# Stick-breaking attention on one NeuronCore: two heads' scores on the two row halves of the matrix array, and one scan over 1280 columns per head

## The chip, the cores and the metric

The kernel runs on one core of one Trainium2 chip. The core has a matrix engine (TensorE, PE in the profile; its weight loads are listed apart as PEld), a vector engine (VectorE, DVE), an activation engine (ScalarE, ACT), a general engine (GpSimd, POOL) and a queue from which most transfers are started (SyncE, SP). Each engine works through its own list of instructions in order. Engines wait for one another through semaphores. Matrix products go to PSUM, which has eight banks of 512 fp32 columns here, and DVE and ACT take them from there to SBUF.

The metric is the device time of one execution in microseconds (us); shorter is better.

## The reference

The program is one layer of a decoder on 512 tokens of width 1024. A normalised input is projected into queries, keys and values of 8 heads of 64, three convolution inputs and two gates. Attention and a gated convolution are mixed, followed by an MLP of width 4096 and a per-layer gate. The part that the change touches is the attention, cut to this (z are the scores of 128 queries against all keys, 4 such blocks):

```
z = einsum('bhqd,bhkd->bhqk', q_block, k) * 64 ** -0.5
causal = key_pos < q_pos
log_beta = log_sigmoid(z)
log_keep = where(causal, log_beta - z, 0)
between = cumsum(log_keep, axis=3, reverse=True) - log_keep
w = where(causal, exp(log_beta + between), 0)
out = einsum('bhqk,bhkd->bhqd', w, v)
```

So the weight of a key is beta = sigmoid(z), times the product of keep = sigmoid(-z) over all later keys that the query may see. The products are taken by a scan from the last key to the first.

## The kernel before

All large products are made from fp32 values that are split in two: `split` (lines 63 to 66) lets ACT copy the value rounded to a shorter format ("hi") and DVE subtract that from the value ("lo"). A product is then three matmuls in one PSUM bank, hi by hi, hi by lo and lo by hi (`mm3`, lines 89 to 92).

Scores have only 64 rows to contract, half of the array's 128. Before, `proj_q` makes for each head a tile `st` with q hi in one half of the rows and q lo in the other. `proj_k` writes k hi into both halves, and k lo into both halves, of the same tile. A score block is then two matmuls over all 128 rows: [q hi; q lo] by [k hi; k hi] (line 338), and [q hi; q lo] by [k lo; k lo] (line 339), which also adds the product lo by lo. This takes six 64-row copies on ACT (lines 315, 317, 325) and six 64-row subtractions on DVE (lines 316, 318, 326) for a pair of heads.

`scores` handles one head. Its keys are cut causally: query block 3 sees 512 columns, block 2 sees 384, block 1 sees 256, block 0 sees 128, together 1280 columns that lie side by side in the tiles `beta` and `keep` (the table `BLK`). ACT makes beta and keep from PSUM in three groups of columns (512, 384 + 128, 256; lines 341 and 342). POOL sets the diagonal blocks (line 347, one 128x128 select for beta and one for keep per query block). For each query block DVE then scans keep backwards (line 350) and multiplies beta by the shifted result (line 351).

The loop over j (line 424, four turns, two heads each) has this order on PE: scores of both heads; `conv_u` and `conv_b` (24 matmuls of 512 columns each); `wtrans` of the first head's weights (ten 128x128 transposes, line 366, which need that head's finished beta); the next q projection; `wtrans` of the second head; the next k projection; two `av`; and the next `conv_c`. In the last turn gates stand in place of the projections. PE and SP run in exactly the written order. For ACT, DVE and POOL a scheduler that works with modelled times and the priorities in the code (`high_priority(-LATE)` marks work that may come late) sets the order when the program is built. Tiles come from pools of a fixed number of buffers: `big` has 16, the weights pool `wts` 15, raw weights 4, PSUM 8.

In the profile every matmul of `mm3` has line 90, 91 or 92, and every split line 64 (ACT) or 65 (DVE), whoever calls them.

Of the kernel before, what the change touches and what calls it, by code (L numbers as in the profile page):

```python
# [16 lines left out]
P = 128  # L17
S = 512
# [10 lines left out]
BLK = {3: (0, 512), 2: (512, 384), 0: (896, 128), 1: (1024, 256)}  # L29
# [4 lines left out]
def hybrid_block(ctx, tc, x, p, g_pre_mix, w_in, b_gate, w_conv, w_attn_out, w_conv_out, w_o,  # L34
                 g_post_mix, g_pre_mlp, w_up, w_down, g_post_mlp, g_ple, w_ple_gate, w_ple_proj, out):
    nc = tc.nc
# [4 lines left out]
    w_in, w_conv, w_attn_out, w_conv_out = w_in[0], w_conv[0], w_attn_out[0], w_conv_out[0]  # L41
# [12 lines left out]
    def bigt(shape, dt=F32R, name="big"):  # L54
        return big.tile(shape, dt, tag="big", name=name)

    def bank():
        return psp.tile([P, 512], F32, tag="ps", name="ps")

    def tm(dt=F32):  # L60
        return tmp.tile([P, 512], dt, tag="tmp", name="tmp")

    def split(hi, lo, src):
        a = nc.scalar.copy(hi, src)  # L64
        b = nc.vector.tensor_tensor(lo, src, hi.bitcast(F32), op=ALU.subtract)  # L65
        return a, b

    def weights(loads, shape):
        raw = raws.tile(shape, F32, tag="raw", name="raw")
        for sel, src in loads(raw):  # L70
            nc.sync.dma_start(sel, src)
        lo = wts.tile(shape, F32R, tag="w", name="wlo")
        hi = wts.tile(shape, F32R, tag="w", name="whi")
        half = shape[1] // 2
        for sl in (slice(0, half), slice(half, 2 * half)):
            split(hi[:, sl], lo[:, sl], raw[:, sl])
        return hi, lo
# [4 lines left out]
    def wcols(w, c0):  # L82
        src = w[:, c0:c0 + P].rearrange("(k p) m -> p k m", p=P)
        return weights(lambda t: [(t, src)], [P, NK, P])
# [4 lines left out]
    def mm3(ps, lh, ll, rh, rl, start, stop, onto=False):  # L89
        nc.tensor.matmul(ps, lh, rh, start=start, stop=False, skip_group_check=onto)  # L90
        nc.tensor.matmul(ps, lh, rl, start=False, stop=False, skip_group_check=onto)  # L91
        nc.tensor.matmul(ps, ll, rh, start=False, stop=stop, skip_group_check=onto)  # L92

    def proj(w, xs, nk=NK, k0=0):
        ps = bank()
        for k in range(nk):
            xh, xl = xs(k)
            mm3(ps, w[0][:, k0 + k], w[1][:, k0 + k], xh, xl, k == 0, k == nk - 1)
        return ps
# [47 lines left out]
    def mov(hp):  # L147
        return lambda k: (hp[0][k // 4][:, k % 4, :], hp[1][k // 4][:, k % 4, :])
# [119 lines left out]
    for t in range(2, NT):  # L268
        ps = bank()
# [11 lines left out]
    hx = mov(h1)  # L281
# [27 lines left out]
        unsaved.extend([(dst[:, 0:2], o[0]), (dst[:, 2:4], o[1])])  # L309


    def proj_q(j):
        a, b = st = [bigt([P, 3, S], name="st") for _ in range(2)]
        ps = proj(wcols(w_in, j * P), hx)
        nc.scalar.copy(a[0:64, 0], ps[0:64])
        nc.vector.tensor_tensor(a[64:128, 0], ps[0:64], a[0:64, 0].bitcast(F32), op=ALU.subtract)
        nc.scalar.copy(b[64:128, 0], ps[64:128])
        nc.vector.tensor_tensor(b[0:64, 0], ps[64:128], b[64:128, 0].bitcast(F32), op=ALU.subtract)
        return st

    def proj_k(j, st):
        ps = proj(wcols(w_in, 512 + j * P), hx)
        for s_, r, o in ((st[0], slice(0, 64), slice(64, 128)), (st[1], slice(64, 128), slice(0, 64))):
            for d in (r, o):
                nc.scalar.copy(s_[d, 1], ps[r])
                nc.vector.tensor_tensor(s_[d, 2], ps[r], s_[r, 1].bitcast(F32), op=ALU.subtract)

    def scores(st):
        beta = bigt([P, 1280], F32, "beta")
        keep = bigt([P, 1280], F32, "keep")  # L330
        for group in ((3,), (2, 0), (1,)):
            ps = bank()
            base = BLK[group[0]][0]
            for qb in group:
                c0, n = BLK[qb]
                c0 -= base
                lhs = st[:, 0, qb * P:(qb + 1) * P]
                nc.tensor.matmul(ps[:, c0:c0 + n], lhs, st[:, 1, 0:n], start=True, stop=False)  # L338
                nc.tensor.matmul(ps[:, c0:c0 + n], lhs, st[:, 2, 0:n], start=False, stop=True)  # L339
            n = sum(BLK[qb][1] for qb in group)  # L340
            nc.scalar.activation(beta[:, base:base + n], ps[:, 0:n], AF.Sigmoid, scale=0.125)
            nc.scalar.activation(keep[:, base:base + n], ps[:, 0:n], AF.Sigmoid, scale=-0.125)
        for qb in (3, 2, 0, 1):
            c0, n = BLK[qb]
            dg = slice(c0 + n - P, c0 + n)
            for t_, fill in ((beta, 0.0), (keep, 1.0)):
                nc.gpsimd.affine_select(t_[:, dg], t_[:, dg], pattern=[[-1, P]], compare_op=ALU.is_gt,
                                        fill=fill, base=0, channel_multiplier=1)
            kr = keep[:, c0:c0 + n][:, ::-1]
            nc.vector.tensor_tensor_scan(kr, kr, kr, 1.0, op0=ALU.mult, op1=ALU.bypass)  # L350
            nc.vector.tensor_tensor(beta[:, c0:c0 + n - 1], beta[:, c0:c0 + n - 1], keep[:, c0 + 1:c0 + n],
                                    op=ALU.mult)
        return beta

    def wtrans(w):
        wh = bigt([P, 1280], name="wth")
        wl = bigt([P, 1280], name="wtl")
        for group in ((0,), (1, 3), (2,)):
            ps = bank()
            base = WBLK[group[0]][0]  # L360
            n = 0
            for kb in group:
                c0 = WBLK[kb][0] - base
                for qb in range(kb, NT):
                    o = BLK[qb][0] + kb * P
                    nc.tensor.transpose(ps[:, c0 + (qb - kb) * P:c0 + (qb - kb + 1) * P], w[:, o:o + P], ident)  # L366
                n += WBLK[kb][1]
            split(wh[:, base:base + n], wl[:, base:base + n], ps[:, 0:n])
        return wh, wl
# [19 lines left out]
    def conv_c(c):  # L389
        ps = proj(wcols(w_in, 2048 + c * P), hx)  # L390
        ct = tm()
        nc.scalar.copy(ct, ps)
        return ct

    def conv_u(c, ct):
        ps = proj(wcols(w_in, 2560 + c * P), hx)
        nc.vector.tensor_tensor(ct, ct, ps, op=ALU.mult)
        y = tm()
        wc = [cols[:, 16 + i * 4 + c:17 + i * 4 + c] for i in range(3)]
        nc.vector.tensor_scalar(y, ct, wc[2], None, op0=ALU.mult)  # L400
        for i, d in ((1, 1), (0, 2)):
            nc.vector.scalar_tensor_tensor(y[:, d:S], ct[:, 0:S - d], wc[i], y[:, d:S], op0=ALU.mult, op1=ALU.add)
        return y

    def conv_b(c, y):
        ps = proj(wcols(w_in, 1536 + c * P), hx)
        nc.vector.tensor_tensor(y, ps, y, op=ALU.mult)
        split(oy_h[1][:, c], oy_l[1][:, c], y)

    def gate(j, which):  # L410
        ps = proj(wcols(w_in, 3072 + 1024 * which + j * P), hx)
        sg = tm()
        nc.scalar.activation(sg, ps, AF.Sigmoid, bias=cols[:, 8 * which + j:8 * which + j + 1])
        return sg

    with tc.high_priority(-LATE):
        make_sums(nc.vector)
    st = proj_q(0)
    with tc.high_priority(-LATE):
        make_sums(nc.vector)  # L420
    proj_k(0, st)
    ct = conv_c(0)
    sg = [None, None]
    for j in range(4):
        wa = scores(st[0])
        wb = scores(st[1])
        y = conv_u(j, ct)
        conv_b(j, y)
        ta = wtrans(wa)
        if j < 3:  # L430
            st = proj_q(j + 1)
        else:
            sg[0] = gate(0, 0)
        tb = wtrans(wb)
        if j < 3:
            proj_k(j + 1, st)
        else:
            sg[1] = gate(0, 1)
        of = tm()
        if j in (1, 2):  # L440
# [20 lines left out]
    for j in range(NK):  # L461
# [28 lines left out]
        if j == 7:  # L490
            for kk in range(2):
                ps = bank()
# [382 lines left out]
    for t in range(2, NT):  # L875
        for cs in CUTS[t]:
            ps = bank()[:, 0:cs.stop - cs.start]
# [31 lines left out]
```

## Time and profile before

| what | value |
|---|---|
| time, median of 3 executions | 736.56 us (735.95 to 737.09) |
| the profiled execution | 737.48 us |
| its span, first to last instruction | 735.7 us |
| PE busy | 727.5 us (99%) |
| DVE busy | 538.4 us (73%) |
| ACT busy | 392.4 us (53%) |
| POOL busy | 89.2 us (12%) |
| granted TensorE clock | 1.000 |
| the four turns of the attention loop | 52.8 to about 195 us of the span |

The timeline view gives for each piece its start, its duration, the engine, the line, the operation with its operands' names and sizes, how many instructions it merges (x4), and in brackets the idle time of the engine before it with what ended it. A matmul's listed duration is a model of its whole way through the array; consecutive matmuls overlap, so the step from one start to the next is what a matmul costs in a stream. The windows view gives for stretches of the span their length and the busy time and count of each engine. The difference of 1.8 us between time and span is what lies around the first and last instruction.

### The profile page before, as it was taken

To read this page: it belongs to the slowest core of one execution; us is meant where nothing else is said; L and a number is where in the kernel's file an instruction comes from. 1 tells how busy PE (TensorE), PEld (TensorE's weight loads), DVE (VectorE), ACT (ScalarE), POOL (GpSimd) and SP (SyncE) were. 2 spreads that over 40 slices of the span, in tenths; PEclk is the share of its full clock that TensorE was granted. 3 is DMA by queue.
4 is the path that set the end of the run, shared out by engine and by line. 5 is a ranking of instruction groups with operands and counts; after the bars stand their busy time and mean duration, and the time that the engine had idled before them with its cause. 6 is when DMAs were issued, how large, how long until landed. Compare 5 with 4: busy or idle time off the path is not lost.

```text
span 735.7 us, 10417 instructions
## 1 busy us (share of the span) xinstructions
PE 727.5 (99%) x3944; PEld 631.4 (86%) x3944; DVE 538.4 (73%) x740; ACT 392.4 (53%) x647; POOL 89.2 (12%) x119
## 2 busy tenths in 40 slices
PE   8999999999999999999999999999999999999997
PEld 7878888888888888888899999999988888888886
DVE  6779898989545533844789898976799878269762
ACT  6264746373434221443856696757767477256431
POOL 1005041323332222001100000000000000001100
PEclk9999999999999999999999999999999999999999
DMA  8591717174798967862325544523555767577311
GB/s 314 170 290 57 218 40 229 62 224 141 234 341 256 279 207 261 296 216 70 152 94 170 176 115 115 148 81 107 153 171 178 219 249 226 177 242 270 128 57 58
DMA packets 112106, 132.29 MB, mean 180 GB/s; under 512 B 4116, under 2 KB 82744, under 8 KB 111032
## 3 DMA queue, kind: packets, MB, share of 16 engines
q1 hardware_dynamic: 111464, 127.43, 54.8%
q10 hardware_dynamic: 592, 4.20, 1.4%
q8 instruction: 31, 0.51, 0.3%
q14 instruction: 19, 0.16, 0.1%
HBM read 108.55 MB, written 23.07 MB: 179 GB/s over the span
## 4 chain that ended last, share of the span: by engine, by line
PE 85%; DVE 6%; DMA 5%; issue 1%; ACT 1%; SPq 0%; POOL 0%; POOLq 0%; DVEq 0%; ACTq 0%
PE ps L90 27%; PE ps L92 27%; PE ps L91 26%; DMA raw<-in_w_up_dram 3%; DMA raw<-in_w_in_dram 2%; DVE us L65 2%; PE ps L380 1%; PE ps L366 1%; PE ps L339 1%; PE ps L181 1%; PE ps L338 1%; PE ps L565 1%; PE ps L140 0%; DVE s L660 0%; DVE wlo L65 0%
## 5 line engine op out<-in xcount | busy, mean ns | idle before, releaser
L65 DVE TENSOR_TENSOR wlo<-raw,whi 128x512 fp32r<-128x512 f32 x120 | 84.8, 737 | 42.7 <-ACT whi L64 20.9
L90 PE MATMUL ps<-h1h,whi 128*128 128x512 f32 x288 | 113.0, 392 | 0.0
L92 PE MATMUL ps<-h1h,wlo 128*128 128x512 f32 x288 | 112.3, 390 | 0.0
L91 PE MATMUL ps<-h1l,whi 128*128 128x512 f32 x288 | 112.2, 390 | 0.0
L64 ACT CAST whi<-raw 128x512 fp32r<-128x512 f32 x120 | 68.9, 630 | 48.5 <-DMA raw<-in_w_in_dram 15.8
L90 PE MATMUL ps<-w,sb 128*128 128x512 f32 x216 | 84.1, 389 | 0.0
L92 PE MATMUL ps<-w,sb 128*128 128x512 f32 x216 | 84.0, 389 | 0.0
L91 PE MATMUL ps<-w,sb 128*128 128x512 f32 x216 | 84.0, 389 | 0.0
L65 DVE TENSOR_TENSOR w<-raw,w 128x1024 fp32r<-128x1024 f32 x56 | 67.6, 1221 | 21.5 <-ACT w L64 10.4
L64 ACT CAST w<-raw 128x1024 fp32r<-128x1024 f32 x56 | 58.4, 1052 | 36.1 <-DMA raw<-wsum 14.4
L132 POOL TENSOR_TENSOR rs<-ms,mhalf 128x1 f32<-128x1 f32 x20 | 14.2, 712 | 419.6 <-DVE ms L128 365.7
L90 PE MATMUL ps<-h2h,us 128*128 128x256 f32 x224 | 63.5, 283 | 0.4 <-DVE tmp L692 0.4
L92 PEld LDWEIGHTS ps<-h1h,wlo 128*128 128x128 f32 x288 | 54.1, 188 | 11.3
L91 PEld LDWEIGHTS ps<-h1l,whi 128*128 128x128 f32 x288 | 54.1, 188 | 10.8
L91 PE MATMUL ps<-h2l,us 128*128 128x256 f32 x224 | 63.4, 283 | 0.0
L92 PE MATMUL ps<-h2h,us 128*128 128x256 f32 x224 | 63.4, 283 | 0.0
L90 PEld LDWEIGHTS ps<-h1h,whi 128*128 128x128 f32 x288 | 54.1, 188 | 10.8
L65 DVE TENSOR_TENSOR us<-raw,us 128x1024 fp32r<-128x1024 f32 x42 | 50.6, 1219 | 5.9 <-ACT us L64 5.8
L64 ACT CAST us<-raw 128x1024 fp32r<-128x1024 f32 x42 | 43.3, 1049 | 17.0 <-DVE raw L664 8.5
L91 PEld LDWEIGHTS ps<-w,sb 128*128 128x128 f32 x216 | 40.6, 188 | 8.4
L92 PEld LDWEIGHTS ps<-w,sb 128*128 128x128 f32 x216 | 40.6, 188 | 8.4
L90 PE MATMUL ps<-tb,us 128*128 128x256 f32 x168 | 47.7, 284 | 0.0
(210 smaller groups left out, 1693.1 us busy)
## 6 DMA issues: line engine op xcount, KB each, us to landing
raw<-in_w_in_dram SPq DMA_DIRECT2D x36, 512.0 KB, 6.5
w<-in_w_down_dram SPq DMA_DIRECT2D x32, 512.0 KB, 4.5
wsum<-w SPq DMA_DIRECT2D x32, 512.0 KB, 4.1
raw<-in_w_up_dram SPq DMA_DIRECT2D x32, 512.0 KB, 4.6
raw<-wsum SPq DMA_DIRECT2D x32, 512.0 KB, 5.0
raw<-in_w_down_dram SPq DMA_DIRECT2D x24, 512.0 KB, 4.2
raw<-in_w_o_dram SPq DMA_DIRECT2D x8, 512.0 KB, 5.7
raw<-in_w_ple_gate_dram SPq DMA_DIRECT2D x8, 512.0 KB, 7.1
```

Source lines behind the costliest of these rows:

```text
L64: a = nc.scalar.copy(hi, src)
L65: b = nc.vector.tensor_tensor(lo, src, hi.bitcast(F32), op=ALU.subtract)
L90: nc.tensor.matmul(ps, lh, rh, start=start, stop=False, skip_group_check=onto)
L91: nc.tensor.matmul(ps, lh, rl, start=False, stop=False, skip_group_check=onto)
L92: nc.tensor.matmul(ps, ll, rh, start=False, stop=stop, skip_group_check=onto)
L132: nc.gpsimd.tensor_tensor(r, m, mhalf, op=ALU.pow)
L181: nc.tensor.transpose(warm[:, 0:P], ident, ident)
L338: nc.tensor.matmul(ps[:, c0:c0 + n], lhs, st[:, 1, 0:n], start=True, stop=False)
L339: nc.tensor.matmul(ps[:, c0:c0 + n], lhs, st[:, 2, 0:n], start=False, stop=True)
L366: nc.tensor.transpose(ps[:, c0 + (qb - kb) * P:c0 + (qb - kb + 1) * P], w[:, o:o + P], ident)
L380: nc.tensor.matmul(ps[:, kb * P:S], lhs, wt[i][:, c0:c0 + n], start=(kb == 0 and i == 0), stop=(kb == NT - 1 and i == 1))
L565: nc.tensor.transpose(ps[:, i * P:(i + 1) * P], hn1[t][g][:, i * P:(i + 1) * P], ident)
```

## The change

q and k are each split once, as one 128-row copy and one 128-row subtraction, into a tile `st` of four parts (q hi, q lo, k hi, k lo). The first head of the pair lies in rows 0 to 63, the second in rows 64 to 127. `scores` handles both heads. Each score block is three matmuls per head with 64 contracted rows (hi by hi, hi by lo, lo by hi), issued alternately for the head in the upper and the head in the lower rows, into two banks. The three column groups of both heads so take six banks. Lo by lo is no longer computed. ACT makes beta and keep of both heads group by group.

A constant tile `ends` holds 1 in the last column of each query block and 0 elsewhere. The scan now goes over all 1280 columns of a head at once: the running product is multiplied by keep, and then the larger of it and `ends` is taken, which starts it again at 1 at each block's last key (where keep has just been set to 1). One multiplication over 1279 columns replaces four; the column at each block's end takes part, where beta is zero on the diagonal.

```diff
     def proj_q(j):
-        a, b = st = [bigt([P, 3, S], name="st") for _ in range(2)]
-        ps = proj(wcols(w_in, j * P), hx)
-        nc.scalar.copy(a[0:64, 0], ps[0:64])
-        nc.vector.tensor_tensor(a[64:128, 0], ps[0:64], a[0:64, 0].bitcast(F32), op=ALU.subtract)
...
+        st = bigt([P, 4, S], name="st")
+        split(st[:, 0], st[:, 1], proj(wcols(w_in, j * P), hx))
         return st

     def proj_k(j, st):
-        ps = proj(wcols(w_in, 512 + j * P), hx)
-        for s_, r, o in ((st[0], slice(0, 64), slice(64, 128)), (st[1], slice(64, 128), slice(0, 64))):
-            for d in (r, o):
-                nc.scalar.copy(s_[d, 1], ps[r])
-                nc.vector.tensor_tensor(s_[d, 2], ps[r], s_[r, 1].bitcast(F32), op=ALU.subtract)
+        split(st[:, 2], st[:, 3], proj(wcols(w_in, 512 + j * P), hx))
...
-                lhs = st[:, 0, qb * P:(qb + 1) * P]
-                nc.tensor.matmul(ps[:, c0:c0 + n], lhs, st[:, 1, 0:n], start=True, stop=False)
-                nc.tensor.matmul(ps[:, c0:c0 + n], lhs, st[:, 2, 0:n], start=False, stop=True)
+                for i, (a, b) in enumerate(((0, 2), (0, 3), (1, 2))):
+                    for h in range(2):
+                        r = slice(64 * h, 64 * h + 64)
+                        nc.tensor.matmul(ps[h][:, c0:c0 + n], st[r, a, qb * P:(qb + 1) * P], st[r, b, 0:n],
+                                         start=i == 0, stop=i == 2)
...
-            kr = keep[:, c0:c0 + n][:, ::-1]
-            nc.vector.tensor_tensor_scan(kr, kr, kr, 1.0, op0=ALU.mult, op1=ALU.bypass)
-            nc.vector.tensor_tensor(beta[:, c0:c0 + n - 1], beta[:, c0:c0 + n - 1], keep[:, c0 + 1:c0 + n],
-                                    op=ALU.mult)
+            kr = keep[h][:, ::-1]
+            nc.vector.tensor_tensor_scan(kr, kr, ends[:, ::-1], 1.0, op0=ALU.mult, op1=ALU.max)
+            nc.vector.tensor_tensor(beta[h][:, 0:1279], beta[h][:, 0:1279], keep[h][:, 1:1280], op=ALU.mult)
...
-        wa = scores(st[0])
-        wb = scores(st[1])
+        wa, wb = scores(st)
```

The scheduler orders ACT, DVE and POOL anew. On ACT, in the second turn of the loop, this is the part from the last copy before the scores to the casts behind them. `beta_868` and `keep_869` are the first head's tiles, `beta_911` and `keep_912` the second's; `whi` are hi parts of weights that PE uses a turn later. Before:

```order
L392 COPY tmp_866<-ps_841 128x512
L341 ACTIVATE beta_868<-ps_870 128x512
L342 ACTIVATE keep_869<-ps_870 128x512
L341 ACTIVATE beta_868<-ps_875 128x512
L342 ACTIVATE keep_869<-ps_875 128x512
L341 ACTIVATE beta_868<-ps_882 128x256
L342 ACTIVATE keep_869<-ps_882 128x256
L341 ACTIVATE beta_911<-ps_913 128x512
```

Now (`beta_852` and `keep_854` belong to the first head, `beta_853` and `keep_855` to the second):

```order
L392 COPY tmp_850<-ps_825 128x512
L64 CAST whi_1318<-raw_1315 128x512 x2
L342 ACTIVATE beta_852<-ps_856 128x512
L343 ACTIVATE keep_854<-ps_856 128x512
L342 ACTIVATE beta_853<-ps_857 128x512
L343 ACTIVATE keep_855<-ps_857 128x512
L64 CAST whi_1376<-raw_1373 128x512
L342 ACTIVATE beta_852<-ps_868 128x512
L343 ACTIVATE keep_854<-ps_868 128x512
L342 ACTIVATE beta_853<-ps_869 128x512
L343 ACTIVATE keep_855<-ps_869 128x512
L342 ACTIVATE beta_852<-ps_886 128x256
```

Three weight casts stand ahead of or among the activations, and the first head's last piece comes ninth and tenth of twelve where it came fifth and sixth. The first and third turn read alike; in the fourth no cast stands between the copy and the last activation.

On DVE, in the same turn, from the last weight subtraction ahead of the first scan to the first convolution product. Before, part of the first head:

```order
L350 SCALAR_TENSOR_TENSOR keep_869<-keep_869 128x512
L351 TENSOR_TENSOR beta_868<-beta_868,keep_869 128x511
L350 SCALAR_TENSOR_TENSOR keep_869<-keep_869 128x384
L350 SCALAR_TENSOR_TENSOR keep_869<-keep_869 128x128
L351 TENSOR_TENSOR beta_868<-beta_868,keep_869 128x383
L351 TENSOR_TENSOR beta_868<-beta_868,keep_869 128x127
L350 SCALAR_TENSOR_TENSOR keep_869<-keep_869 128x256
L350 SCALAR_TENSOR_TENSOR keep_912<-keep_912 128x512
L351 TENSOR_TENSOR beta_868<-beta_868,keep_869 128x255
```

Now, all of both heads (a scan is named SCALAR_TENSOR_TENSOR here):

```order
L65 TENSOR_TENSOR wlo_1317<-raw_1315,whi_1318 128x512 x2
L351 SCALAR_TENSOR_TENSOR keep_854<-keep_854,ends_383 128x1280
L351 SCALAR_TENSOR_TENSOR keep_855<-keep_855,ends_383 128x1280
L352 TENSOR_TENSOR beta_852<-beta_852,keep_854 128x1279
L352 TENSOR_TENSOR beta_853<-beta_853,keep_855 128x1279
L397 TENSOR_TENSOR tmp_850<-tmp_850,ps_942 128x512
```

Both scans stand ahead of both multiplications, so the first head's weights are finished behind the second head's scan. All four turns have this order.

More of the change, by code (lines that the diff above doesn't have):

```diff
@@ L309, in make_sums @@
         unsaved.extend([(dst[:, 0:2], o[0]), (dst[:, 2:4], o[1])])
+    ends = bigt([P, 1280], F32, "ends")
+    nc.gpsimd.memset(ends, 0.0)
+    for c0, n in BLK.values():
+        nc.gpsimd.memset(ends[:, c0 + n - 1:c0 + n], 1.0)
     def proj_q(j):
-        a, b = st = [bigt([P, 3, S], name="st") for _ in range(2)]
-        ps = proj(wcols(w_in, j * P), hx)
-        nc.scalar.copy(a[0:64, 0], ps[0:64])
-        nc.vector.tensor_tensor(a[64:128, 0], ps[0:64], a[0:64, 0].bitcast(F32), op=ALU.subtract)
-        nc.scalar.copy(b[64:128, 0], ps[64:128])
-        nc.vector.tensor_tensor(b[0:64, 0], ps[64:128], b[64:128, 0].bitcast(F32), op=ALU.subtract)
+        st = bigt([P, 4, S], name="st")
+        split(st[:, 0], st[:, 1], proj(wcols(w_in, j * P), hx))
         return st
     def proj_k(j, st):
-        ps = proj(wcols(w_in, 512 + j * P), hx)
-        for s_, r, o in ((st[0], slice(0, 64), slice(64, 128)), (st[1], slice(64, 128), slice(0, 64))):
-            for d in (r, o):
-                nc.scalar.copy(s_[d, 1], ps[r])
-                nc.vector.tensor_tensor(s_[d, 2], ps[r], s_[r, 1].bitcast(F32), op=ALU.subtract)
+        split(st[:, 2], st[:, 3], proj(wcols(w_in, 512 + j * P), hx))
     def scores(st):
-        beta = bigt([P, 1280], F32, "beta")
-        keep = bigt([P, 1280], F32, "keep")
+        beta = [bigt([P, 1280], F32, "beta") for _ in range(2)]
+        keep = [bigt([P, 1280], F32, "keep") for _ in range(2)]
         for group in ((3,), (2, 0), (1,)):
-            ps = bank()
+            ps = [bank(), bank()]
             base = BLK[group[0]][0]
@@ L336, in scores @@
                 c0 -= base
-                lhs = st[:, 0, qb * P:(qb + 1) * P]
-                nc.tensor.matmul(ps[:, c0:c0 + n], lhs, st[:, 1, 0:n], start=True, stop=False)
-                nc.tensor.matmul(ps[:, c0:c0 + n], lhs, st[:, 2, 0:n], start=False, stop=True)
-            n = sum(BLK[qb][1] for qb in group)
-            nc.scalar.activation(beta[:, base:base + n], ps[:, 0:n], AF.Sigmoid, scale=0.125)
-            nc.scalar.activation(keep[:, base:base + n], ps[:, 0:n], AF.Sigmoid, scale=-0.125)
@@ L343, in scores @@
[L343 to L348, printed above, removed]
-            kr = keep[:, c0:c0 + n][:, ::-1]
-            nc.vector.tensor_tensor_scan(kr, kr, kr, 1.0, op0=ALU.mult, op1=ALU.bypass)
-            nc.vector.tensor_tensor(beta[:, c0:c0 + n - 1], beta[:, c0:c0 + n - 1], keep[:, c0 + 1:c0 + n],
-                                    op=ALU.mult)
+                for i, (a, b) in enumerate(((0, 2), (0, 3), (1, 2))):
[3 more added lines that the diff above has]
+                                         start=i == 0, stop=i == 2)
@@ new lines, in scores @@
+            n = sum(BLK[qb][1] for qb in group)
+            for h in range(2):
+                nc.scalar.activation(beta[h][:, base:base + n], ps[h][:, 0:n], AF.Sigmoid, scale=0.125)
+                nc.scalar.activation(keep[h][:, base:base + n], ps[h][:, 0:n], AF.Sigmoid, scale=-0.125)
+        for h in range(2):
+            for c0, n in BLK.values():
+                dg = slice(c0 + n - P, c0 + n)
+                for t_, fill in ((beta[h], 0.0), (keep[h], 1.0)):
+                    nc.gpsimd.affine_select(t_[:, dg], t_[:, dg], pattern=[[-1, P]], compare_op=ALU.is_gt,
+                                            fill=fill, base=0, channel_multiplier=1)
+            kr = keep[h][:, ::-1]
+            nc.vector.tensor_tensor_scan(kr, kr, ends[:, ::-1], 1.0, op0=ALU.mult, op1=ALU.max)
+            nc.vector.tensor_tensor(beta[h][:, 0:1279], beta[h][:, 0:1279], keep[h][:, 1:1280], op=ALU.mult)
```

## The prediction

> **What bounds the kernel now.** I read the page's busy times first, then the chain of waits, then the four turns of the attention loop in the windows and timeline views.
>
> ```profile
> PE 727.5 (99%) x3944; PEld 631.4 (86%) x3944; DVE 538.4 (73%) x740; ACT 392.4 (53%) x647; POOL 89.2 (12%) x119
> PE 85%; DVE 6%; DMA 5%; issue 1%; ACT 1%; SPq 0%; POOL 0%; POOLq 0%; DVEq 0%; ACTq 0%
> ```
>
> PE is busy for 99% of the span and makes 85% of the chain. So the change can gain only by giving PE less to do, or by removing one of its few waits. Work taken from DVE and ACT is worth nothing by itself; a result of theirs that comes later than PE wants it costs its full lateness. The change touches one stretch of each turn: from the first score matmul to the first transpose of the first head's weights (line 366). The windows view, one row per turn (length, then busy time and count by engine):
>
> ```profile
> 52.77:68.46 15.69, 14.61 (x67) 11.67 (x67) 13.92 (x22) 9.90 (x21) 9.79 (x16) 1.00 0.24 87
> 89.42:102.89 13.47, 13.47 (x65) 11.34 (x64) 12.04 (x20) 8.83 (x19) 9.32 (x16) 1.00 0.25 91
> 124.02:137.50 13.48, 13.48 (x66) 11.35 (x65) 12.05 (x20) 8.83 (x19) 9.32 (x16) 1.00 0.22 83
> 158.61:172.10 13.49, 13.49 (x66) 11.35 (x65) 11.94 (x21) 6.84 (x16) 9.16 (x16) 1.00 0.39 117
> ```
>
> In the last three turns PE never stops in it. In the first it does. I call the moment when PE is free for the scores T0, and the first transpose T1. PE in the second turn, then in the first:
>
> ```profile
> 89.42 0.39 PE L338 MATMUL ps<-st 128*128 128x512 f32 x1
> ...
> 90.68 0.40 PE L338 MATMUL ps<-st 128*128 128x512 f32 x1
> ...
> 91.96 0.39 PE L90 MATMUL ps<-h1h,whi 128*128 128x512 f32 x1
> ...
> 102.89 1.25 PE L366 MATMUL ps<-ident,beta 128*128 128x128 f32 x10
> ```
> ```profile
> 52.54 0.39 PE L92 MATMUL ps<-h1h,wlo 128*128 128x512 f32 x1
> 52.82 0.51 PE L338 MATMUL ps<-st 128*128 128x512 f32 x1
> ...
> 55.50 0.50 PE L338 MATMUL ps<-st 128*128 128x512 f32 x1 [0.64 <-ACT st L325]
> ...
> 57.37 0.40 PE L90 MATMUL ps<-h1h,whi 128*128 128x512 f32 x1
> ...
> 68.30 0.27 PE L366 MATMUL ps<-ident,beta 128*128 128x128 f32 x1
> ```
>
> In the second turn scores take 91.96 - 89.42 = 2.54 us, conv_u and conv_b 102.89 - 91.96 = 10.93. In the first T0 is about 52.77 (52.54 plus a step of 0.23), scores last until 57.37, 4.60 us: about 2.06 us of waiting for the 64-row splits. T1 is 68.30.
>
> **The change part by part.** *The splits.* Six copies and six subtractions a turn become two of each.
>
> ```profile
> L326 DVE TENSOR_TENSOR st<-ps,st 64x512 fp32r<-64x512 f32 x16 | 11.0, 687 | 4.6 <-ACT st L325 4.3
> ```
>
> That takes 4 x 0.69 = 2.7 us a turn off DVE (ACT about as many pieces less), and in turns two to four nobody waited for them. In the first turn one copy and one subtraction follow the k projection, which PE ends 24 matmuls before T0; both are done before T0. So the 2.06 us of waiting go, if nothing later takes them back.
>
> *The matmuls.* One head's share above is 91.96 - 90.68 = 1.28 us for two matmuls per block, so one pass over all blocks costs 0.64. Now there are six passes of half height. If two heads' matmuls run side by side, three passes count: 1.92 us, and that is the lower end, since every column must stream. If they run one after another, six count: 3.84. The trace has no pair of half-height matmuls on opposite halves, so both ends stay; I take 1.92, since the two share neither rows nor banks. Entering and leaving the half-height form costs something, bounded by the nearest case, a transpose of 28 rows between full ones:
>
> ```profile
> 35.83 0.39 PE L92 MATMUL ps<-vh,h1l 128*128 128x512 f32 x1
> 36.14 0.24 PE L278 MATMUL ps<-ident,crow 28*128 28x28 f32 x1
> 36.31 0.50 PE L90 MATMUL ps<-h1h,whi 128*128 128x512 f32 x1
> 36.65 0.40 PE L91 MATMUL ps<-h1l,whi 128*128 128x512 f32 x1
> ```
>
> From 35.83 to 36.65 pass 0.82 us for two steps of 0.23 and 28 columns (about 0.03): 0.33 us too much, taken once per turn; the other end is zero. Scores: 1.92 + 0.33 = 2.25 us, and PE would reach T1 at T0 + 2.25 + 10.93 = T0 + 13.18, which is 0.29 less than 13.47.
>
> [...]
>
> *The first head's weights.* This is the term that decides. ACT in the second turn of before:
>
> ```profile
> 89.62 0.59 ACT L392 COPY tmp<-ps 128x512 f32<-128x512 f32 x1 [1.32 <-PE ps L92]
> 90.14 0.60 ACT L341 ACTIVATE beta<-ps 128x512 f32<-128x512 f32 x1
> ...
> 92.06 0.41 ACT L341 ACTIVATE beta<-ps 128x256 f32<-128x256 f32 x1
> 92.33 0.43 ACT L342 ACTIVATE keep<-ps 128x256 f32<-128x256 f32 x1
> ...
> 95.03 2.28 ACT L64 CAST whi<-raw 128x512 fp32r<-128x512 f32 x4
> ```
>
> Copy at T0 + 0.20, next instruction at + 0.72; a 512-column activation steps (92.06 - 90.14)/4 = 0.48, a 256-column one 0.27, a weight cast 2.28/4 = 0.57. In the new order: two casts to 1.86, four activations to 3.78, a cast to 4.35, four activations to 6.27; the first head's last keep starts at 6.54 and ends near 7.0. POOL, then DVE's groups, then DVE in the second turn:
>
> ```profile
> 91.29 0.29 POOL L347 TENSOR_SCALAR_AFFINE_SELECT keep<-keep 128x128 f32<-128x128 f32 x1 [0.19 <-ACT keep L342]
> 91.78 1.95 POOL L347 TENSOR_SCALAR_AFFINE_SELECT beta<-beta 128x128 f32<-128x128 f32 x2 [0.20 <-ACT beta L341]
> 93.68 0.54 POOL L347 TENSOR_SCALAR_AFFINE_SELECT keep<-keep 128x128 f32<-128x128 f32 x2
> ```
> ```profile
> L350 DVE TENSOR_TENSOR_SCAN keep<-keep 128x512 f32<-128x512 f32 x8 | 10.0, 1249 | 2.9 <-POOL keep L347 2.9
> ...
> L350 DVE TENSOR_TENSOR_SCAN keep<-keep 128x128 f32<-128x128 f32 x8 | 3.6, 446 | 0.0
> ...
> L65 DVE TENSOR_TENSOR w<-raw,w 128x1024 fp32r<-128x1024 f32 x56 | 67.6, 1221 | 21.5 <-ACT w L64 10.4
> ```
> ```profile
> 91.62 1.23 DVE L350 TENSOR_TENSOR_SCAN keep<-keep 128x512 f32<-128x512 f32 x1 [0.93 <-POOL keep L347]
> 92.88 0.69 DVE L351 TENSOR_TENSOR beta<-beta,keep 128x511 f32<-128x511 f32 x1
> ...
> 102.23 0.41 DVE L351 TENSOR_TENSOR beta<-beta,keep 128x255 f32<-128x255 f32 x1
> ```
>
> Selects take 0.27 to 0.29 us while no scan runs (1.95 for two while one does). In the new order no scan runs before the first head's last select, so POOL keeps up: the four selects behind the last 512-column keep end near 7.5, and the scan starts 0.04 later (91.58 to 91.62), at T0 + 7.6. A scan grows by (1249 - 446)/384 = 2.09 ns a column; 1280 columns take 1.249 + 768 x 0.00209 = 2.85 us, about 2.8 from start to start. A product of 1279 columns takes 1.221 + 255 x 0.00104 = 1.49 (slope from 0.69 at 511 to 1.221 at 1024). DVE runs scan, scan, product: 7.6 + 2.8 + 2.8 + 1.49 = T0 + 14.7, and with the semaphore and an uncovered weight load T1 = T0 + 14.8. Before, the first head was done long ahead and even the second ended at 102.64, T0 + 13.2. So PE now waits about 1.6 us at line 366, and a turn's stretch is 14.8 - 13.47 = 1.3 us longer.
>
> *The sum.* Second and third turn: +1.3 each. First turn: T1 = 52.77 + 14.8 = 67.6 instead of 68.30, -0.7: the new wait eats two thirds of the old one. It rests on two loads being there: casts at 53.5 and 56.6 read transfers issued at
>
> ```profile
> 45.83 0.37 SPq L71 DMA_DIRECT2D raw<-in_w_in_dram  x1
> 47.88 0.37 SPq L71 DMA_DIRECT2D raw<-in_w_in_dram  x1
> 43.69 7.31 DMA raw<-in_w_in_dram
> ```
>
> and 7.31 us, as the one issued at 43.69 took, brings them in at 53.1 and 55.2, just in time. Fourth turn: no cast stands between, which takes 3 x 0.57 = 1.7 us off the chain; 13.1 hides behind PE's 13.18, so -0.3. Together -0.7 + 1.3 + 1.3 - 0.3 = +1.6 us.
>
> What follows on DVE is later by some 2.8 us in the waiting turns (16.1 against 13.2), while PE is later by 1.3. The next thing PE could miss is the bank of conv_b, freed by line 407: the second product ends near T0 + 16.1, and nine instructions of about 0.6 us (the weight subtractions' and conv's, as 0.69 and 0.41 above) stand from there through line 407, so I get it at about T0 + 21.5, and the k projection wants it at about T0 + 22.4 (14.8, two sets of ten transposes of 1.0 to 1.1, one projection of 5.5). Cover of 0.9 us; beyond it PE waits again. The memsets of `ends` lie on POOL far before its first select. Behind the loop PE has no slack (99%), so I carry the shift through unchanged. The profiled execution took 737.48 us, 1.8 around its span of 735.7: 737.48 + 1.6 = 739.1. It lies 0.9 above the median of 736.56, so against the runs I predict 736.56 + 1.6 = 738.2. A measurement of this kernel can tell about 0.2%, 1.5 us, from no change; the forecast stands right on that line.
>
> **The rivals.** *The chain hides* (faster). If the first head's weights are ready when PE arrives, only the gain stays: first turn 52.77 + 13.18 = 65.95 against 68.30, -2.35, and 3 x -0.29: -3.2 us, 733.3. For it: DVE has 2.7 us less to do a turn. Against it: the order puts two scans ahead of the product; each would have to take under (13.18 - 7.6 - 1.5)/2 = 2.0 us, and the slope gives 2.85. Halfway (stalls of half the size) is no change.
>
> *The halves run one after another* (slower). Scores cost 3.84 + 0.33 = 4.17, T1 = T0 + 15.1, which hides DVE's chain. First turn -0.4, the others +1.6 each: +4.5, 741.1. For it: nothing in the trace ran side by side. Against: different rows, different banks.
>
> *The wait moves on* (slower). If the scan with its second operation, or DVE's backlog, is slower by more than the 0.9 us of cover, PE waits at lines 366 and again for conv_b's bank; one more column-step per scan (3.1 ns) gives 4.1 us a scan, T1 near T0 + 17.4, +3.9 in two turns, +1.9 and +2.2 in the others: +12, 748. Nothing in the profile speaks for it but that no scan with two operations stands there.
>
> **How the numbers follow.** Forecast (side by side, PE waits in turns two and three) 0.56; one after another 0.16; hidden 0.14; between hidden and forecast 0.08; wait moves on 0.06. The forecast's own range is +0.3 to +2.8 (a tenth of a microsecond or two in each of ten steps, in three turns): 736.9 to 739.4. Under half of it lies above 1.5 us. Slower: 0.26 + 0.16 + 0.06 = 0.48. Faster: 0.14 less a little, 0.13. Within: 0.39. The range runs from 735.0 (most of the hidden case is left out) to 741.7 (one after another is in, the moved wait is out).
>
> **What would show it.** Right: PE idle of about 1.5 us ahead of line 366 (the same number in the changed file) released by DVE's 1279-column product (its line 352), in the second and third turn and not in the fourth; no wait for `st` in the first; scans near 2.85 us; score matmuls of 64 rows in pairs that start together; the span to T1 near 14.8 us. Wrong: no idle there (hidden), score stretches near 4 us (one after another), or waits of PE for a bank ahead of the k projection.

## The result and the profile after

The changed kernel took 743.64 us (median of five executions, 740.80 to 745.19) against 736.56 (735.95 to 737.23): slower by a factor of 1.0086, 95% interval 1.0057 to 1.0116 (estimated from all executions, so not the quotient of the medians). The medians differ by 7.1 us, where +1.6 was predicted; the sign is right, the size is not, and the time lies above the predicted range. The profiled execution is the fastest of the five, 740.80 us for a span of 739.1. The page's busy times and its chain of waits:

```profile
PE 726.8 (98%) x3976; PEld 628.8 (85%) x3976; DVE 518.9 (70%) x676; ACT 382.0 (52%) x631; POOL 82.3 (11%) x124
PE 85%; DVE 5%; POOL 4%; DMA 3%; ACT 1%; issue 1%; SPq 1%; POOLq 0%; DVEq 0%; ACTq 0%
```

DVE, ACT and POOL have less to do than before: 19.5, 10.4 and 6.9 us. (PE's 0.7 us less says little, since a second profile of the kernel before reads 726.8 too.) Yet the span grew by 3.4 us, and POOL, which had no share of the chain, now has 4%. What grew is PE's idle time: 739.1 - 726.8 = 12.3 us against 735.7 - 727.5 = 8.2. PE's waits (releaser: total, times, longest) show where, and the windows of the four turns, each from T0 to T1 (the last two rows end 0.02 and 0.04 us short of it), when:

```profile
PE ps L366 <- DVE beta L352: 5.9, 4, 2.1
```
```profile
52.91:68.45 15.54, 13.39 (x73) 10.82 (x73) 9.92 (x8) 8.81 (x19) 7.54 (x16) 1.00 0.27 94
89.61:104.37 14.76, 13.39 (x74) 10.82 (x73) 9.80 (x8) 8.80 (x19) 6.89 (x16) 1.00 0.17 59
125.56:140.60 15.04, 13.38 (x73) 10.79 (x73) 9.86 (x8) 8.82 (x19) 7.52 (x16) 1.00 0.18 61
161.79:175.80 14.01, 13.38 (x73) 10.78 (x72) 8.85 (x7) 7.68 (x17) 7.08 (x16) 1.00 0.50 150
```

PE waits for the first head's product in all four turns. From T0 to T1 the stretches were 15.53, 13.47, 13.48 and 13.49 us (the row of 15.69 in the prediction runs 0.16 us past T1, which is at 68.30); they are 15.54, 14.76, 15.06 and 14.05, together 3.4 us more. PE in the first turn, and its first transposes in the second:

```profile
52.68 0.39 PE L92 MATMUL ps<-h1h,wlo 128*128 128x512 f32 x1
53.00 2.19 PE L338 MATMUL ps<-st 64*128 64x512 f32 x24
55.13 0.50 PE L90 MATMUL ps<-h1h,whi 128*128 128x512 f32 x1
...
68.45 1.28 PE L366 MATMUL ps<-ident,beta 128*128 128x128 f32 x10 [2.15 <-DVE beta L352]
...
104.37 1.28 PE L366 MATMUL ps<-ident,beta 128*128 128x128 f32 x10 [1.37 <-DVE beta L352]
```

The scores did become cheaper: from T0 = 52.68 + 0.23 = 52.91 to the next projection at 55.13 are 2.22 us for both heads, where the second turn of before took 2.54, and nobody waits for `st`. What PE waits for shows in DVE's groups: the scan's eight calls have 14.1 us of idle time ahead of them, until the last select of a head:

```profile
L351 DVE TENSOR_TENSOR_SCAN keep<-keep,ends 128x1280 f32<-128x1280 f32 x8 | 22.8, 2855 | 14.6 <-POOL keep L348 14.1
L352 DVE TENSOR_TENSOR beta<-beta,keep 128x1279 f32<-128x1279 f32 x8 | 11.5, 1475 | 0.0
```

Before, the scans of single blocks began with the first block. The same group in a second profile of the kernel before:

```profile
L350 DVE TENSOR_TENSOR_SCAN keep<-keep 128x512 f32<-128x512 f32 (+3 forms) x32 | 26.5, 858 | 4.6 <-POOL keep L347 4.6
```

This explains 3.4 of the 7.1 us. The rest needs two more facts, found below: the profile of before that the prediction used had 1.8 us of a wait that a second profile, near the median, does not have; and six of ten executions of the changed kernel are slower at a lower mean clock of TensorE, which one profile shows halved for 3.4 us.

### The profile page after: what moved, and what is told of

Same layout as the page of the kernel before. It is cut to its first block, busy times and chain, and to the rows that moved or that the text cites. A ratio compares the mean times of both kernels' runs of the same rounds, so it can differ in the third digit from the quotient of the medians.

```text
span 739.1 us, 10383 instructions
## 1 busy us (share of the span) xinstructions
PE 726.8 (98%) x3976; PEld 628.8 (85%) x3976; DVE 518.9 (70%) x676; ACT 382.0 (52%) x631; POOL 82.3 (11%) x124
## 4 chain that ended last, share of the span: by engine, by line
PE 85%; DVE 5%; POOL 4%; DMA 3%; ACT 1%; issue 1%; SPq 1%; POOLq 0%; DVEq 0%; ACTq 0%
PE ps L90 27%; PE ps L91 27%; PE ps L92 27%; POOL keep L348 2%; DMA raw<-in_w_in_dram 2%; DVE keep L351 2%; PE ps L380 1%; PE ps L366 1%; POOL beta L348 1%; DVE beta L352 1%; PE ps L181 1%; DVE vl L65 1%; DMA wsum<-w 1%; PE ps L564 1%; DVE wlo L65 1%
```

## The experiments

**The changed kernel again**, for a second profile and five more times.

> The changed kernel unchanged. Five executions took 740.8 to 745.2 us, and the profiled one, at 740.8, waits 5.9 us at line 366 (2.15, 1.37, 1.68, 0.67 in the four turns) at a clock of 0.999. Theory A (the stalls also make TensorE's clock drop in some executions): again a spread of 3 to 5 us; an execution above 742 shows a mean clock under 0.999, and (1 - clock) x 743 us gives most of its excess over 740.8; a profile that hits one shows stretches at a lower clock right behind a wait at line 366. Theory B (transfers that come later in some executions lengthen ScalarE's queue and with it the stalls): the same spread at a clock of 1.000, and a profile that hits one shows longer idle time at line 366 and of ScalarE for a transfer.

Median 742.39 us (741.37 to 743.82, a spread a little under the 3 to 5 us expected) against 735.80 for 23 executions of before on the same chip: 1.0094 (1.0081 to 1.0107). Of the ten executions now at hand, the four with a mean clock of 0.999 or 1.000 took 740.80, 740.96, 741.37 and 741.69 us, on average 741.2. The six with 0.994 to 0.998 took 742.39 to 745.19, on average 743.9. Their lower mean clocks (0.9968 against 0.9998) make about 2.2 of these 2.7 us, as an estimate. A mean of 0.998 alone proves no drop, for two executions of the kernel before have it too; but this profile (743.82 us, clock 0.998) shows one. Two windows of it, and PE there:

```profile
66.60:70.01 3.41, 1.05 (x10) 0.97 (x10) 3.41 (x3) 0.00 (x0) 0.00 (x0) 1.00 0.44 154
70.01:73.42 3.41, 3.41 (x12) 2.73 (x10) 3.41 (x7) 0.00 (x0) 0.00 (x0) 0.50 0.00 0
```
```profile
69.07 1.49 PE L366 MATMUL ps<-ident,beta 128*128 128x128 f32 x10 [2.36 <-DVE beta L352]
...
70.79 0.63 PE L91 MATMUL ps<-h1l,whi 128*128 128x512 f32 x1
71.22 0.63 PE L92 MATMUL ps<-h1h,wlo 128*128 128x512 f32 x1
```

Right behind the wait of 2.36 us the clock is 0.50 for 3.41 us, and matmuls step by 0.43 us instead of 0.23. By these steps that costs about 3.41 / 2 = 1.7 (an estimate) of the 3.0 us by which this execution lies above 740.80, so theory A holds for the larger part. Theory B has a share: in the first and third turn ScalarE's cast between the sigmoids stands 0.90 and 0.63 us for a transfer, where the first profile has 0.66 and 0.19, and the stalls there grow from 2.15 and 1.68 to 2.36 and 2.09 us.

**VectorE in the order scan, product, scan, product.**

```
-            kr = keep[h][:, ::-1]
-            nc.vector.tensor_tensor_scan(kr, kr, ends[:, ::-1], 1.0, op0=ALU.mult, op1=ALU.max)
-            nc.vector.tensor_tensor(beta[h][:, 0:1279], ...)
+            with tc.issue_after(done.ins) if h else nullcontext():
+                nc.vector.tensor_tensor_scan(keep[h][:, ::-1], keep[h][:, ::-1], ends[:, ::-1], ...)
+            done = nc.vector.tensor_tensor(beta[h][:, 0:1279], ...)
```

> The changed kernel, with the second head's scan queued behind the first head's product, so VectorE runs scan, product, scan, product. Theory A (the wait at line 366 is the second scan's 2.85 us standing ahead of the first product): the product ends 2.8 us earlier, near T0 + 11.9 in the second turn, PE's work of 13.1 us hides it, the 5.9 us of waits at line 366 go, and the later k projection, now wanted near T0 + 20.7 instead of 22.4, waits up to 1 us for the bank that line 407 frees at about T0 + 20.8 to 21.5. Time 733 to 735, clock 1.000 and a spread under 1.5 us, as before the change. Rival C (the transposes wait for what ScalarE and GpSimd deliver, and the order of the scans is no matter): time stays near 741 and the waits at line 366 stay over 4 us. Rival D (the drop of the clock comes from the 64-row matmuls, not from the stalls): the spread of 4 us and clocks of 0.994 to 0.998 stay although the waits are gone.

735.41 us (11 executions, 734.62 to 736.98), ratio 0.9995 (0.9985 to 1.0005); clocks 0.998 to 1.000. The time is 0.4 us above the expected 733 to 735. PE's window in the first turn from the first score matmul, which starts 0.09 us after T0, to T1 (13.15 in the other three too), DVE in the second, and PE at the first turn's k projection:

```profile
52.59:65.74 13.15, 13.15 (x74) 10.92 (x74) 7.82 (x7) 8.82 (x19) 7.38 (x16) 1.00 0.25 91
```
```profile
94.80 2.89 DVE L351 TENSOR_TENSOR_SCAN keep<-keep,ends 128x1280 f32<-128x1280 f32 x1 [4.14 <-POOL keep L348]
97.72 1.49 DVE L352 TENSOR_TENSOR beta<-beta,keep 128x1279 f32<-128x1279 f32 x1
99.13 2.82 DVE L351 TENSOR_TENSOR_SCAN keep<-keep,ends 128x1280 f32<-128x1280 f32 x1
```
```profile
73.81 0.50 PE L90 MATMUL ps<-h1h,whi 128*128 128x512 f32 x1 [0.26 <-DVE tmp L407]
```

The product now ends at 97.72 + 1.49 = 99.21, T0 + 11.8, and PE arrives at T0 + 13.24 without a stop. The whole wait at line 366 was the second scan standing ahead of the first product. The matmuls are those of the changed kernel, and yet one execution of eleven has a mean clock of 0.998 and none a lower one (of the kernel before, two of 43 have 0.998), so rival D falls: the lower clocks (down to 0.994 in the changed kernel) go with the stalls, not with the 64-row form. Two short waits for the bank that line 407 frees (0.26 us here, about 0.3 in the third turn) take its place, as the prediction's 0.9 us of cover suggested. Against before this is no change.

**The three matmuls of a block not alternating between the heads** (with the order just shown).

```
-                for i, (a, b) in enumerate(((0, 2), (0, 3), (1, 2))):
-                    for h in range(2):
+                for h in range(2):
+                    for i, (a, b) in enumerate(((0, 2), (0, 3), (1, 2))):
```

> As the reordered kernel, but in each block the three matmuls of the first head come before the three of the second, so that neighbours on TensorE mostly share a row half (only the pairs at a change of head lie on opposite halves). If halves run at once only when neighbours lie on opposite halves: one of each six overlaps, so the group of 24 matmuls takes about (24 - 4) / 4 x 0.64 + 0.33 = 3.5 us to 4.2 us instead of 2.13; time about 4 x 1.4 to 4 x 2 = 5 to 8 us above the reordered kernel's if nothing hides it. If the halves overlap in any order: 2.1 to 2.3 us and the same time.

735.19 us (10 executions), 0.9992 (0.9983 to 1.0001). The score matmuls of the first turn:

```profile
53.01 2.20 PE L338 MATMUL ps<-st 64*128 64x512 f32 x24
```

The changed kernel has 2.19 us there, and the window to T1 is that of the reordered kernel, 13.15. In this run halves that stand three places apart in the queue still run at once. So this kernel doesn't price the serial case. That the pairs overlap is shown by the 2.2 us for six passes of which three alone take 1.92, and by the starts in the trace of the changed kernel: the two matmuls of a pair start 3 or 4 ns apart, in all 48 pairs. Here the first two score matmuls make one piece of 0.50 us, as the first pair does there; a 512-column matmul a step of 0.23 us behind another, at 0.39 us each, would make 0.62. That also rules out that a half-height matmul merely takes half as long.

**Two more passes of VectorE ahead of the first product.**

```
             kr = keep[h][:, ::-1]
+            for _ in range(2 - 2 * h):
+                nc.vector.tensor_tensor(beta[0], beta[0], beta[0], op=ALU.max)
```

> The changed kernel with two more passes of VectorE over the first head's 1280 columns ahead of its product (each the maximum of the tile with itself, some 1.5 us, which changes no value). Theory A: each pass goes straight into the waits at line 366: 1.2 to 1.5 us each, so some 2.7 us a turn, waits near 4.8, 4.0, 4.3 and 3.3 us and 740.8 + 11 = 752 at an undisturbed clock; and if stalls make the clock drop, more executions and longer stretches show it: mean clock 0.98 to 0.995 and up to 6 us more. If stalls do not touch the clock: 752, clock as in the changed kernel or higher. If the wait at line 366 were not VectorE's chain: under 745.

758.82 us (6 executions, 754.16 to 760.58), 1.0302 (1.0275 to 1.0328), clocks 0.985 to 0.995. PE's waits (the product is line 354 here, the transposes line 368), and windows around all four of them (length, busy time by engine, granted clock ahead of the last two columns):

```profile
PE ps L368 <- DVE beta L354: 16.3, 4, 5.3
```
```profile
64.40:67.81 3.41, 1.76 (x8) 1.13 (x6) 3.41 (x3) 0.00 (x0) 1.43 (x1) 1.00 0.17 36
67.81:71.22 3.41, 0.00 (x0) 0.00 (x0) 3.41 (x3) 0.00 (x0) 0.00 (x0) 1.00 0.29 118
71.22:74.63 3.41, 3.19 (x13) 3.03 (x14) 3.41 (x6) 0.00 (x0) 0.00 (x0) 0.50 0.00 0
...
108.77:112.18 3.41, 0.84 (x8) 0.88 (x9) 3.41 (x3) 0.12 (x1) 0.00 (x0) 1.00 0.35 136
112.18:115.59 3.41, 3.41 (x12) 2.82 (x10) 3.38 (x7) 1.74 (x4) 0.00 (x0) 0.50 0.00 0
...
146.31:149.72 3.41, 1.21 (x6) 0.67 (x4) 3.41 (x2) 0.00 (x0) 0.00 (x0) 1.00 0.34 114
149.72:156.55 6.83, 4.87 (x17) 4.33 (x18) 6.80 (x10) 1.97 (x4) 0.00 (x0) 0.50 0.05 20
...
187.27:190.69 3.42, 1.26 (x6) 0.72 (x4) 3.42 (x2) 0.00 (x0) 0.00 (x0) 1.00 0.00 0
190.69:197.51 6.82, 5.98 (x19) 5.17 (x20) 6.79 (x10) 2.48 (x5) 0.00 (x0) 0.50 0.01 2
```

The waits grew by 16.3 - 5.9 = 10.4 us, 2.6 a turn as expected, which gives 741.2 + 10.4 = 751.6 at full clock; the other 7 us go with the halved clock, which in this execution follows every one of the four stalls, for 20.5 us in all.

**The kernel before again**, for a second profile of it.

> The kernel before, unchanged, for a second profile. The profiled execution that the prediction rests on took 737.48 us; 23 more executions have a median of 735.8. In that profile ScalarE's cast at 51.02 stood 1.92 us for its transfer, the 64-row splits came behind it, and PE idled about 1.8 us in the first turn. Theory A (that wait belongs to that one execution): a profile with a time near 735.8 has a first stretch of under 14.7 us instead of 15.69, PE waits for the splits of under 1 us in all, and no wait of ScalarE for a transfer over 1 us there. Rival B (the wait is in every execution): the stretch is 15.3 to 15.8 us again, and the 1.7 us lie elsewhere.

736.06 us (10 executions), profiled at 735.94, span 734.2. The first stretch (the other three are 13.47), and ACT ahead of the scores, here and then in the first profile:

```profile
52.85:66.59 13.74, 13.72 (x65) 11.32 (x64) 12.65 (x21) 9.31 (x20) 9.78 (x16) 1.00 0.26 96
```
```profile
49.31 1.14 ACT L64 CAST whi<-raw 128x512 fp32r<-128x512 f32 x2
```
```profile
51.02 1.14 ACT L64 CAST whi<-raw 128x512 fp32r<-128x512 f32 x2 [1.92 <-DMA raw<-in_w_in_dram]
```

In the first profile the cast stood 1.92 us for its transfer and ran at 51.02, with the splits behind it; here it runs at 49.31 without a wait, the splits are early, and the stretch is 13.74 us instead of 15.53. Theory A holds: the wait that the change removes in the first turn is 13.74 - 13.47 = 0.27 us in this execution, not 2.06.

**The long scan alone**, on the kernel before (old splits and scores).

```
-            kr = keep[:, c0:c0 + n][:, ::-1]
-            nc.vector.tensor_tensor_scan(kr, kr, kr, 1.0, op0=ALU.mult, op1=ALU.bypass)
-            nc.vector.tensor_tensor(beta[:, c0:c0 + n - 1], ...)
+        kr = keep[:, ::-1]
+        nc.vector.tensor_tensor_scan(kr, kr, ends[:, ::-1], 1.0, op0=ALU.mult, op1=ALU.max)
+        nc.vector.tensor_tensor(beta[:, 0:1279], beta[:, 0:1279], keep[:, 1:1280], op=ALU.mult)
```

> The kernel before with its old splits and scores, one head after the other, and only the scan over 1280 columns with the marks. Theory A (the long scan hurts only where the second head's scan is ready before the first head's product is issued): here VectorE runs scan, product, scan, product, the first product ends near T0 + 9, some 4 us ahead of PE's T0 + 13.47, and the time is that of before within 1 us at a clock of 1.000, without a wait at the transposes. Rival: the long scan is itself too late for PE: waits of over 1 us ahead of the transposes and 739 or more.

739.53 us (739.05 to 740.02), 1.0045 (1.0032 to 1.0058). Neither expectation: no wait at the transposes, clocks of 0.999 to 1.000, and yet 3.5 us slower. PE's waits, then DVE in the second turn (scan is line 355), then the same `wtl` in the kernel before, then PE at its product with the values (line 384):

```profile
PE ps L384 <- DVE wtl L65: 2.0, 2, 1.0
```
```profile
91.60 2.89 DVE L355 TENSOR_TENSOR_SCAN keep<-keep,ends 128x1280 f32<-128x1280 f32 x1 [1.65 <-POOL keep L352]
...
97.42 2.83 DVE L355 TENSOR_TENSOR_SCAN keep<-keep,ends 128x1280 f32<-128x1280 f32 x1 [1.41 <-POOL keep L352]
...
114.08 1.29 DVE L308 TENSOR_TENSOR w<-w,w 128x512 f32<-128x512 f32 x2 [0.29 <-PE ps L91]
...
116.01 1.60 DVE L65 TENSOR_TENSOR wtl<-ps,wth 128x512 fp32r<-128x512 f32 x3
```
```profile
111.86 1.29 DVE L65 TENSOR_TENSOR wtl<-ps,wth 128x512 fp32r<-128x512 f32 x2
```

```profile
115.32 0.44 PE L384 MATMUL ps<-wth,v 128*128 128x512 f32 x1
116.74 0.50 PE L384 MATMUL ps<-wtl,v 128*128 128x512 f32 x1 [0.98 <-DVE wtl L65]
```

DVE stands 3.1 us for the two heads' last selects, and the low part of the second head's transposed weights is begun at 116.01, where the kernel before begins it at 111.86. PE (last fence) wants it a step of 0.23 after 115.32 and gets it at 116.74. The second and third turn each take 1.5 us more than in the second profile of before, which is 3.0 of the 3.5 us. Part of the delay is the order in which the program was laid out: here three subtractions of the weight sums (line 308) stand ahead of `wtl`, and before they stand behind it. How much of the 3.5 us is the later scan and how much this order was not separated.

**The split and the side by side scores alone**, with the old scan of each block.

```
-            kr = keep[h][:, ::-1]
-            nc.vector.tensor_tensor_scan(kr, kr, ends[:, ::-1], 1.0, op0=ALU.mult, op1=ALU.max)
-            nc.vector.tensor_tensor(beta[h][:, 0:1279], ...)
+                kr = keep[h][:, c0:c0 + n][:, ::-1]
+                nc.vector.tensor_tensor_scan(kr, kr, kr, 1.0, op0=ALU.mult, op1=ALU.bypass)
+                nc.vector.tensor_tensor(beta[h][:, c0:c0 + n - 1], ...)
```

> The changed kernel's one split and its scores side by side, with the old scan of each block. [...] Rival (the side by side scores alone put the first head too late): waits of 1 to 2 us a turn ahead of the transposes and 739 to 742, with clocks under 0.999 in some executions.

734.84 us (11 executions, 734.45 to 735.83) against 736.06 for 20 of before: 0.9981 (0.9973 to 0.9990), the only kernel here whose interval lies below 1. Its first window, again from the first score matmul (the others are 13.15 too), its scans (line 347) and PE's wait at the transposes (line 363):

```profile
52.74:65.89 13.15, 13.15 (x74) 10.93 (x73) 10.42 (x15) 8.80 (x19) 8.61 (x16) 1.00 0.22 84
...
L347 DVE TENSOR_TENSOR_SCAN keep<-keep 128x512 f32<-128x512 f32 (+3 forms) x32 | 26.7, 857 | 4.8 <-POOL keep L344 4.8
...
PE ps L363 <- DVE beta L348: 0.5, 1, 0.5
```

In the last three turns the first head is ready in time, and what PE saves shows: from T0, 13.47 - 13.24 = 0.23 us in each. In the first turn PE stops once among the transposes for 0.5 us, where the rival expects 1 to 2. The author's estimate had been waits of 0 to 0.5 us a turn and 734.5 to 737 us, from 8.8 us of scans and products up to the first head's end and an allowance for GpSimd's selects, which in the profile before took 0.29 to 0.30 us with VectorE idle and up to 1.21 us beside a scan. The four turns together are about 0.5 us shorter than in the second profile of before; where the rest of the 1.2 us comes from is not shown.

## Why the prediction was half right

**Right, within 0.2 us: the mechanism and its sizes in the second turn.** Scores 2.25 us predicted, 2.22 measured; PE's path 13.18, measured 13.24 where nothing stops it; scan 2.85 and product 1.49, measured 2.855 and 1.475; the first scan's start T0 + 7.6, measured 97.01 - 89.61 = 7.4; T1 at T0 + 14.8, measured 14.76. The cover of 0.9 us for conv_b's bank held too. DVE, then PE, in the second turn:

```profile
97.01 5.83 DVE L351 TENSOR_TENSOR_SCAN keep<-keep,ends 128x1280 f32<-128x1280 f32 x2 [4.67 <-POOL keep L348]
...
110.38 0.68 DVE L407 TENSOR_TENSOR tmp<-ps,tmp 128x512 f32<-128x512 f32 x1
```
```profile
111.98 0.47 PE L90 MATMUL ps<-h1h,whi 128*128 128x512 f32 x1
```

Line 407 ends at 111.06, 0.92 us ahead of the k projection. The rival of one half after the other is out (2.2 us, not 4.17), and so is the moved wait. That the halves run side by side was the author's choice between 1.92 and 3.84 us; the 2.22 us measured show it.

**Wrong: "So the 2.06 us of waiting go".** This term was mis-sized by 1.8 us. The wait was real in the profile but belonged to that execution's late transfer; the one profiled near the median, at 735.94, has 0.27. The prediction even held the hint: its profile lay 0.9 us above the median shown, and the cast that stood 1.92 us for a transfer was in it. Adding the same 1.6 to 737.48 and to the median of 736.56 carried a saving that the median never had. With 13.74 as the first turn's old length, its term is 14.8 - 13.74 = +1.1 instead of -0.7, and the sum 3.4 instead of 1.6.

**Wrong: the first and the fourth turn's chain.** ACT and the queue of transfers in the first turn; then ACT, POOL and DVE in the fourth:

```profile
57.36 0.62 ACT L64 CAST whi<-raw 128x512 fp32r<-128x512 f32 x1 [0.66 <-DMA wsum<-w]
```
```profile
49.78 2.20 SPq L291 DMA_DIRECT2D wsum<-w  x2
```
```profile
162.93 0.60 ACT L342 ACTIVATE beta<-ps 128x512 f32<-128x512 f32 x1 [0.37 <-PE ps L338]
...
167.03 0.48 ACT L343 ACTIVATE keep<-ps 128x256 f32<-128x256 f32 x1
```
```profile
168.14 0.30 POOL L348 TENSOR_SCALAR_AFFINE_SELECT keep<-keep 128x128 f32<-128x128 f32 x1
```
```profile
168.48 5.83 DVE L351 TENSOR_TENSOR_SCAN keep<-keep,ends 128x1280 f32<-128x1280 f32 x2 [2.40 <-POOL keep L348]
```

In the first turn the cast between the sigmoids waits 0.66 us, and the stretch is 15.54, not 14.8. It is not one of the two loads that the prediction called "just in time": the last load of `raw` ahead of it, issued at 49.37, landed at 54.8. The profile names a store of weight sums, `wsum<-w`, the second of the two above, which landed at 57.3. The sums lie in the pool `wts`, from which the cast's `whi` takes its buffer, so the likely reason is that the buffer was not free yet; the prediction has no such wait. In the third turn the same cast waits 0.19 us for such a store, and the stretch is 15.06. In the fourth turn the prediction took three casts, 1.7 us, off the chain and hid the rest ("13.1 hides behind PE's 13.18, so -0.3"). Two things stand behind the casts that it didn't price. Without them ACT reaches its first sigmoid before PE has the scores, and waits (162.93 is T0 + 1.14, where the sum let it start at 0.72). And POOL, which takes both heads' selects in one queue, becomes the chain: the first head's last `keep` starts on ACT at 167.03, its select only at 168.14. So the scan starts at T0 + 6.69 instead of 5.9, T1 is T0 + 14.05, and the turn costs +0.6 instead of -0.3. With these, the four stretches are 59.4 us against 54.15 in the second profile of before: +5.3, and the executions at full clock say 741.2 - 735.8 = +5.4.

**Missing: what a stall does to the clock.** The prediction carried each stall at its own length, and its sum has no term for the clock. Six of ten executions took on average 743.9 - 741.2 = 2.7 us more, about 2.2 of it by their lower clock, which takes the median from 741.2 to 742.4 in one set and to 743.6 in the other. So the miss of 743.6 - 738.2 = 5.4 us is, within 0.1, 1.8 for the first turn's old wait, 1.9 (5.3 - 3.4) for the chains and 2.4 for these slower executions, mostly the clock, less 0.8 by which the two medians of before differ.

**The forecast's rivals.** "The chain hides" gave 733.3 and needed scans under 2.0 us; the reordered kernel makes it come true by order instead, and its time is 735.4, since 2.35 of that rival's 3.2 us were mostly the same first-turn wait.

## What to carry over

Merging four short instructions into one long one saved busy time here (22.8 us for eight scans, 26.5 for 32) and still cost. The long scan starts when the last of its inputs is there (14.1 us of waiting for POOL ahead of eight, 4.6 ahead of 32), and its product starts behind its end (a scan of 2.89 us from 94.80, the product at 97.72). Where the next engine wants the first part early, keep the pieces, or at least see that no second long instruction stands ahead of what the first one feeds.

A wait in one profile is a saving only if it is in the usual execution too: where the profiled time lies above the median, look for the wait that makes it so, and leave it out of the sum.

## What the runs showed of the hardware

A stall of TensorE can cost more than its length: in the dosed kernel 10.4 us more of waiting went with 758.82 - 741.2 = 17.6 us more of time. Apart from the first 10 us of the program (in the changed kernel 128-column matmuls step by 0.21 us there and by 0.11 right behind) and its idle end, the clock is halved in these traces for 3.41 us or 6.83 us, from moments that fit a grid of 3.41 us (in the dosed kernel 71.22, 112.18, 149.72 and 190.69, whose distances are 12, 11 and 12 times 3.413). It followed grid windows in which PE, as the windows view models it, was busy for 0.00, 0.84, 1.05, 1.21 and 1.26 of 3.41 us; it didn't follow 1.76 us in the dosed kernel. The nearest miss is the changed kernel's first stall, 2.15 us long, in the grid window

```profile
64.84:68.25 3.41, 1.47 (x7) 0.89 (x5) 3.41 (x3) 0.00 (x0) 0.00 (x0) 1.00 0.27 65
```

which shows 1.47 us busy; the clock stayed at 1.00 in the next. The same stall, 0.2 us longer and otherwise placed on the grid, did halve the clock in the second profile. So the length of a stall and its place on the grid seem to decide together, which would give one kernel executions with and without the drop; this is the author's reading of the windows above, and no run varied one of the two alone. The windows of 0.84 and 1.05 us hold mostly transposes, those of 1.21 and 1.26 us none, so the clock halved behind windows of either kind. The busiest window behind which it halved is 37% busy (1.26 of 3.41 us), the least busy of these behind which it did not is 43% busy (1.47).

Matmuls on opposite row halves overlapped also when they were three places apart in the queue (24 score matmuls in 2.20 us, against 2.19 where the heads alternate), so alternating them by hand brought nothing (735.41 us with it, 735.19 without).
